# Splits of the fourth weight rows behind pair two's sums, pair three's tokens a step later, and two output scalings of the last pairs in another place

## The chip, the core and the metric

The kernel runs on one core of a Trainium2 chip. Five engines work side by side: TensorE multiplies matrices, VectorE (DVE in the profile) and ScalarE (ACT) work on tiles, GpSimd (POOL) does the small per-token numbers and some transfers, SyncE (SP) issues most transfers. Each engine runs its own instructions strictly in order and waits where an operand, a buffer or a transfer isn't ready. The metric is the device time of one execution in microseconds (us). The kernel before took 1026.99 us, the median of 3 runs (1026.68 to 1027.75).

## The reference, cut to what matters

One layer of a hybrid decoder: 2048 prompt tokens of width 1024 and 8 decode tokens. All is in fp32.

```python
def mixer_layer(x, pos, s_ret, s_hg, norm_g, w_in, ret_g, hg_g, lb, w_out):
    h = rmsnorm(x, norm_g)
    p = (h @ w_in).astype(jnp.float32)
    rq, rk, rv, rg, hq, hf, hi, hgate = jnp.split(p, 8, axis=-1)
    ...
    o_ret, s_ret_new = chunked_decay_recurrence(rq, rk, rv, log_gamma, s_ret)
    o_ret = head_rmsnorm(o_ret, ret_g) * jax.nn.silu(rg)
    ...
    o_hg, s_hg_new = chunked_decay_recurrence(hq_act, kin, hi, logf, s_hg)
    o_hg = head_rmsnorm(o_hg, hg_g) * jax.nn.silu(hgate)
    o_cat = jnp.concatenate([o_ret, o_hg], axis=-1).astype(x.dtype)
    y = x + o_cat @ w_out
    return y, s_ret_new, s_hg_new

y_prompt = rmsnorm(mixer_layer(x_prompt, ...), final_norm_g)
```

Two places matter here. The first is the value columns of `h @ w_in`, the first product that the kernel makes. The last is `x + o_cat @ w_out` with the final norm behind it, which ends the program.

## The kernel before, in words

**Number format.** Every fp32 operand of a product is split into a high and a low part. `hi_lo` (L116 to 118) does this: ScalarE copies the operand into a rounded tile (L117, names that end in `h`), and VectorE subtracts that from the operand (L118, names that end in `l`). `three` (L348 to 352) then issues three matmuls for every 128 rows of depth: high by high, high by the weight's low part, low by high.

**Pairs and seven products.** The prompt is worked in 8 pairs of two 128-token chunks. For a pair, tokens and weights form a 2 by 2 block product. It takes seven products in place of eight, in the order of `CHAIN` (L354): A11·B11 into bank a, A12·B21 into b, S2·T2 into a, S1·T1 into c, S3·T3 into a, S4·B22 into c, A22·T4 into a. A11 to A22 are blocks of the scaled tokens, S1 to S4 sums of them, B11 to B22 blocks of the weights, T1 to T4 sums of those. Each product is 12 matmuls of 512 columns. Banks a and c are used again within a pair: `keep` (L388 to 390) copies a bank's contents to SBUF with ScalarE after the first products (tiles `s`, `u`, `p`), and `emit` (L392) copies or adds out the finished results (L402, L403, L405).

**The first pairs.** Pairs 0 and 1 are done as eight plain products. Pair 2 is the first with seven, so the sums of the weights must stand ready by then. `wr[k]` are the rows of the weight as loaded, 8 blocks of 128; blocks `k` and `k + 4` meet in `wv_comb(k)` (L510), which makes T2, T3, T1, T4 by four VectorE subtractions in place (`w_sums`, L504 to 507) and splits each. `wv_comb(3)` (L688) makes the fourth such set. In pair 1's loop over its four banks, pair 2's tokens are prepared: `spread(2)` (L282) lays the norm factors of the tokens across the partitions (the copy at L290, tile `rb`); `tok_ops` (L295) scales eight token blocks with VectorE (L302), splits A (`ab_h`, `ab_l`; first A11 with 512 columns, then A12 and A22 together with 1024), and makes the sums S (L318 s1, L319 s2, L320 s3, L321 s4; s2 and s3 lie in one tile, s1 and s4 in another); `s_split` (L328) splits one of these tiles: `s20h`, `s20l` for S2 and S3, `s21h`, `s21l` for S1 and S4. SP stores the scaled tokens and the sums to DRAM for later passes (L312, L324).

**The loop over the further pairs.** From pair 2 on (L928 onward), work for other pairs is hung behind a pair's products: `after[n]` is called when the instructions of product n are written. In the program before, behind product 2 of pair `i` stand `tok_ops(i + 1)` and the split of its first sums, behind product 4 the split of the second; `tok_load(i + 2)` (L237) stands behind product 2 as well. For `i == 2` also `decode_values_out` (L609) stands behind product 3: four ScalarE copies of the decode tokens' values (L615) and two scalings (L616). `stats_sum` (L269) squares token rows `xn` on ScalarE for the norm factors.

**What sets the order.** TensorE's order is written out by hand. On the other engines a scheduler places each instruction. `behind(f)` (L126) holds what `f` issues behind the instructions last written on VectorE, ScalarE and SP, and `queued(f, engines)` (L1714) does so for the engines named.

**The output product.** At the end, `o_pair(i)` (L1799) makes the same seven products for `o_cat @ w_out`, in the order 0, 1, 2, 4, 5, 6, 3 (the last pair: 0, 1, 2, 4, 5, 3, 6). VectorE adds the results into the tiles `xro` of the pair's two chunks `ca` and `cb`, which hold `x` (loads at L1763, three buffers). `y_sq` squares them on ScalarE (L1767), `y_rs` makes the norm factor on GpSimd (L1770, L113, L114), and `y_out` (L1794) scales the finished 1024 columns on VectorE (L1796) and has GpSimd store them (L1797). A buffer of `xro` is free for the next load when that store is done. The last pair is put out in halves (`y_half`, L1789).

Of the kernel before, what the change touches and what calls it, by code (L numbers as in the profile page):

```python
# [14 lines left out]
ALU = mybir.AluOpType  # L15
# [26 lines left out]
def step_kernel(ctx, tc, a, out):  # L42
# [467 lines left out]
    def wv_comb(k):  # L510
        for op, r in w_sums(wr[k], wr[k + 4]):
            h, l = wv(op, k)
            hi_lo(h, l, r)

    def wg_load(n, k):
        for j, kk in enumerate((k, k + 4)):
            if n == 1 and (j or k % 2):
                tags = (f"zh{j}", f"zl{j}") if k % 2 else ("rk", "rg")
                wr[kk] = [vq.tile([P, GW], F32, tag=t, name=f"wgr{n}{kk}{t}") for t in tags]
                for g, r in enumerate(wr[kk]):  # L520
                    sp.dma_start(r, a[f"w_{n}"][kk, :, g * GW : (g + 1) * GW])
            else:
                wr[kk] = rawp.tile([P, 2, GW], F32, tag="raw", name=f"wgr{n}{kk}")
                sp.dma_start(wr[kk].rearrange("p g n -> p (g n)"), a[f"w_{n}"][kk])
# [160 lines left out]
    wv_comb(1)  # L685
    tok_load(2)
    wv_comb(2)
    wv_comb(3)  # L688
    for ty in (1, 0):
        for c in range(2):  # L690
            ps = bank([P, GW], f"pv1{c}{ty}")
            for k in range(KT):
                plain_k(1, ps, c, ty, k, k == 0, k == KT - 1)
            plain_out(1, c, ty, ps)
            if (c, ty) == (0, 0):
                spread(2)
                held = []
                stats_load(3, 0)
                stats_sum(3, 0)
                stats_load(3, 1)  # L700
                tok_ops(2, held, lambda: stats_sum(3, 1))
                stats_end(3)
                tok_load(3)
                for f in held:
                    f()
                s_split(2, 0)
    s_split(2, 1)
    stats_load(4, 0)
    dve.tensor_tensor(lbd, lbraw[:, :, 0], lbraw[:, :, 1], op=ALU.subtract)
    act.activation(lb, lbd, AF.Sigmoid)  # L710
# [208 lines left out]
    for i in range(2, n_tok):  # L919
# [16 lines left out]
        elif i + 1 < n_tok:  # L936
            if not spooled(i + 1):
                after[1] += [lambda i=i: spread(i + 1)]
            tied = behind if i >= N_V - 1 else lambda f: f()
            late = 2 if same(i) else 0  # L940
            after[2 + late] += [
                lambda i=i, t=tied: t(lambda: tok_ops(i + 1)), lambda i=i, t=tied: t(lambda: s_split(i + 1, 0))
            ]
            after[4 + late // 2] += [lambda i=i, t=tied: t(lambda: s_split(i + 1, 1))]
        if i + 2 < n_tok and not same(i + 2):
            at = 5 if i % N_V > 2 else 2
            if same(i + 1):
                at = 6
            after[at] += [lambda i=i: tok_load(i + 2)]
# [844 lines left out]
    def y_out(c, ms):  # L1794
        rows = slice(c * P, (c + 1) * P)
        dve.scalar_tensor_tensor(xro[c], xro[c], ms[:, 0:1], fg, op0=ALU.mult, op1=ALU.mult)  # L1796
        pool.dma_start(out["y_prompt"][0, rows, :], xro[c])  # L1797

    def o_pair(i, after):  # L1799
        ca, cb = 2 * i, 2 * i + 1  # L1800
        last = cb == T // P - 1
        box = {}
        lo, hi = slice(0, GW), slice(GW, D)
        ms = {c: sm.tile([P, 2], F32, tag="yms", name=f"yms{c}") for c in (ca, cb)}
# [5 lines left out]
        for step, n in enumerate((0, 1, 2, 4, 5, 3, 6) if last else (0, 1, 2, 4, 5, 6, 3)):  # L1810
# [11 lines left out]
                y_sq(ca, lo, ms[ca][:, 0:1])  # L1822
            elif n == 2:
                dve.tensor_tensor(keep("u2"), ps, box["s1"], op=ALU.add)  # L1824
            elif n == 4:
                dve.tensor_tensor(keep("u4"), ps, box["u2"], op=ALU.add)  # L1826
                dve.tensor_tensor(xa[:, hi], xa[:, hi], box["u4"], op=ALU.add)  # L1827
                dve.tensor_tensor(xb[:, hi], xb[:, hi], box["u4"], op=ALU.add)  # L1828
            elif n == 5:
                dve.tensor_tensor(xa[:, hi], ps, xa[:, hi], op=ALU.add)  # L1830
                y_sq(ca, hi, ms[ca][:, 1:2])
                y_rs(ms[ca])
                if not last:
                    y_out(ca, ms[ca])
                dve.tensor_tensor(xb[:, lo], xb[:, lo], box["u2"], op=ALU.add)  # L1835
            elif n == 3:
                dve.tensor_tensor(xb[:, hi], ps, xb[:, hi], op=ALU.add)
                dve.tensor_tensor(xb[:, lo], ps, xb[:, lo], op=ALU.add)
                if last:
                    y_sq(cb, hi, ms[cb][:, 0:1], D ** -0.5)  # L1840
                    pool.tensor_scalar(ms[cb][:, 0:1], ms[cb][:, 0:1], 1.0, EPS, op0=ALU.mult, op1=ALU.add)
                    queued(lambda: y_half(ca, ms[ca], hi), (dve,))
                else:
                    y_sq(cb, hi, ms[cb][:, 0:1])
                    y_sq(cb, lo, ms[cb][:, 1:2])
# [158 lines left out]
```

## Time and profile before

| | |
|---|---|
| median of 3 runs | 1026.99 us (1026.68 to 1027.75) |
| profiled execution's own time | 1027.67 us |
| its span, first to last instruction | 1025.8 us |
| TensorE granted clock, mean | 0.999 |
| busy: TensorE, VectorE, ScalarE, GpSimd | 1014.7, 734.3, 551.5, 126.3 us |
| DMA traffic | 255.63 MB, mean 249 GB/s |

The profiled execution has its own time, 1.9 us longer than its span: what lies before the first and behind the last instruction. A row of a timeline has start, length, engine, line, operation, output and inputs, sizes, the count of instructions in the row, and in brackets the engine's idle time just ahead with what ended it. A row with a count covers all its instructions from the first start to the last end. On TensorE and VectorE a listed length overlaps the start of the next instruction: in a run without waits, a 512-column matmul starts every 0.23 us though its row says 0.39. "PEclk" in a window is the share of TensorE's full clock that was granted.

### The profile page before, as it was taken

What the parts mean: (1) busy time and instruction counts of PE and PEld (TensorE: products, weight loads), DVE (VectorE), ACT (ScalarE), POOL (GpSimd) and SP (SyncE); (2) the same over time, 40 slices, a digit from 0 to 9 for tenths busy, and PEclk for the clock granted to TensorE, in tenths of its full rate; (3) what the DMA queues carried; (4) which work ended last, traced back from release to release, by engine and by line L of the source; (5) the groups of instructions that cost most, each with busy time, mean ns of one, the idle gap of its engine ahead of it and who ended that gap; (6) DMA issues with size and microseconds to landing.
All of it is one profiled execution on the core that took longest, in us unless ns stands there. A gap on an engine that the chain in (4) does not pass through costs nothing. (4 is left out here: it accounts for less than half of the span.)

```text
span 1025.8 us, 21565 instructions
## 1 busy us (share of the span) xinstructions
PE 1014.7 (99%) x8372; PEld 842.6 (82%) x8372; DVE 734.3 (72%) x1353; ACT 551.5 (54%) x1211; POOL 126.3 (12%) x231
## 2 busy tenths in 40 slices
PE   9999999999999999999999999999999999999996
PEld 8767778887778888888888899898888878887775
DVE  5897665988675885566666758768768576668886
ACT  6864335735434665555564655666556476433242
POOL 0210101000000101111111100111022112301122
PEclk9999999999999999999999999999999999999999
DMA  8688998768999975677776697655963497566652
GB/s 288 219 303 312 371 341 310 302 251 315 319 323 307 363 250 165 190 244 240 226 239 193 220 328 260 205 178 205 288 205 133 136 350 234 180 254 205 231 183 103
DMA packets 152135, 255.63 MB, mean 249 GB/s; under 512 B 11520, under 2 KB 79376, under 8 KB 151904
## 3 DMA queue, kind: packets, MB, share of 16 engines
q1 hardware_dynamic: 142232, 225.01, 64.7%
q0 software_dynamic: 7440, 24.76, 6.3%
q10 hardware_dynamic: 2360, 4.47, 1.2%
q8 instruction: 66, 1.08, 0.4%
q14 instruction: 37, 0.30, 0.1%
HBM read 166.51 MB, written 87.69 MB: 248 GB/s over the span
## 5 line engine op out<-in xcount | busy, mean ns | idle before, releaser
L1054 PE MATMUL pjfh<-xh,w_h 128*128 128x512 f32 (+2 forms) x160 | 59.4, 371 | 0.0
L1054 PE MATMUL pjqh<-xh,w_h 128*128 128x512 f32 (+2 forms) x160 | 58.7, 367 | 0.0
L1248 ACT ACTIVATE kepth<-kh 128x1024 f32<-128x1024 f32 x24 | 25.4, 1060 | 60.4 <-DVE kh L1238 60.4
L1054 PE MATMUL pjfh<-xl,w_h 128*128 128x512 f32 (+2 forms) x160 | 55.7, 348 | 0.0
L1054 PE MATMUL pjqh<-xh,w_l 128*128 128x512 f32 (+2 forms) x160 | 55.7, 348 | 0.0
L1054 PE MATMUL pjfh<-xh,w_l 128*128 128x512 f32 (+2 forms) x160 | 55.6, 348 | 0.0
L1054 PE MATMUL pjqh<-xl,w_h 128*128 128x512 f32 (+2 forms) x160 | 55.6, 347 | 0.0
L1238 DVE TENSOR_TENSOR kh<-kh,fph 128x512 f32<-128x512 f32 x48 | 33.4, 696 | 22.7 <-PE plh L1268 19.7
L118 DVE TENSOR_TENSOR ab_l<-xr,ab_h 128x512 fp32r<-128x512 f32 (+1 forms) x40 | 37.4, 954 | 14.1 <-ACT ab_h L117 14.1
L783 DVE SCALAR_TENSOR_TENSOR obr<-por,omr,rg 128x128 f32<-128x128 f32 x64 | 18.0, 344 | 31.9 <-POOL omr L775 24.9
L773 ACT ACTIVATE obr<-por 128x128 f32<-128x128 f32 x64 | 16.9, 278 | 44.1 <-PE por L760 40.3
L117 ACT ACTIVATE ab_h<-xr 128x512 fp32r<-128x512 f32 (+1 forms) x40 | 32.3, 839 | 8.4 <-DVE xr L302 8.4
L1054 PEld LDWEIGHTS pjqh<-xh,w_h 128*128 128x128 f32 x160 | 30.4, 190 | 4.8 <-issue 1.2
L1054 PEld LDWEIGHTS pjfh<-xh,w_h 128*128 128x128 f32 x160 | 30.2, 189 | 4.1 <-issue 0.4
L1054 PEld LDWEIGHTS pjqh<-xh,w_l 128*128 128x128 f32 x160 | 30.1, 188 | 4.0
L1054 PEld LDWEIGHTS pjfh<-xh,w_l 128*128 128x128 f32 x160 | 30.1, 188 | 4.0
L409 ACT ACTIVATE vo<-vo 128x512 f32<-128x512 f32 x32 | 20.1, 629 | 23.7 <-DVE vo L403 10.5
L1241 DVE TENSOR_TENSOR qqh<-qqh,fph 128x512 f32<-128x512 f32 x48 | 32.8, 683 | 0.0
L1054 PEld LDWEIGHTS pjqh<-xl,w_h 128*128 128x128 f32 x160 | 30.2, 189 | 3.0
L1054 PEld LDWEIGHTS pjfh<-xl,w_h 128*128 128x128 f32 x160 | 30.2, 189 | 2.7
L302 DVE SCALAR_TENSOR_TENSOR xr<-xr,g_in,rb 128x256 f32<-128x256 f32 x64 | 26.9, 479 | 2.6 <-DMA xr<-in_x_t 2.4
L1681 PE MATMUL py<-woh,oc_h 128*128 128x512 f32 x64 | 26.7, 417 | 0.0
(1877 smaller groups left out, 3347.0 us busy)
## 6 DMA issues: line engine op xcount, KB each, us to landing
xr<-a_dram SPq DMA_DIRECT2D x24, 512.0 KB
S<-s_dram SPq DMA_DIRECT2D x24, 512.0 KB
xn<-in_x_prompt SPq DMA_DIRECT2D x32, 256.0 KB
xr<-in_x_t SPq DMA_DIRECT2D x16, 512.0 KB
a_dram<-xr SPq DMA_DIRECT2D x16, 512.0 KB
s_dram<-S SPq DMA_DIRECT2D x16, 512.0 KB
xr<-a_dram SPq DMA_DIRECT2D x32, 256.0 KB
or<-o_dram SPq DMA_DIRECT2D x16, 512.0 KB
```

What stands on the lines that cost most here:

```text
L117: act.activation(h, src, AF.Copy)
L118: dve.tensor_tensor(l, src, h.bitcast(F32), op=ALU.subtract)
L302: dve.scalar_tensor_tensor(r[:, k], r[:, k], g_in[:, kk : kk + 1], spread_to[i], op0=ALU.mult, op1=ALU.mult)
L409: act.activation(o, src, AF.Silu)
L773: act.activation(o[:, cc], po[:, h], AF.Square, scale=P ** -0.5, accum_out=ms[:, h : h + 1])
L783: dve.scalar_tensor_tensor(o[:, cc], po[:, h], ms[:, h : h + 1], rb_of[c, "g"][:, cc], op0=ALU.mult, op1=ALU.mult)
L1054: pe.matmul(ps, ww[:, kk], x[:, k, b0 : b0 + n], start=(k == 0 and i == 0), stop=(k == KT - 1 and i == 2),)
L1238: dve.tensor_tensor(kv[:, :, 0, :], kv[:, :, 0, :], two[:, :, 1:2].to_broadcast([P, nb, b]), op=ALU.mult)
L1241: dve.tensor_tensor(qv[:, :, 1, :], qv[:, :, 1, :], two[:, :, 0:1].to_broadcast([P, nb, b]), op=ALU.mult)
L1248: act.activation(ss[:, 512:], k[:, :HALF], AF.Copy)
L1681: pe.matmul(ps, o[:, kk], w[:, k % 4, i * 512 : (i + 1) * 512], start=(k == 0 and n == 0), stop=(k == KT - 1 and n == 2),)
```

## The change

It has three parts.

First, the fourth set of weight sums. `wv_comb_two(3)` makes three of the four subtractions and splits T2 where `wv_comb(3)` stood. T1's split is given to `behind` after the split of pair 2's first sums, and T3's split, the fourth subtraction and T4's split to `behind` after the split of the second.

Second, for `i == 2` the token work of pair 3 and its first split stand behind product 3 in place of 2, and `tok_load(4)` likewise. The second split stays behind product 4.

Third, in pair 6 the scaling and the store of chunk 12 are queued on VectorE behind the additions of product 3, and those of chunk 13 are kept for the last pair, queued behind its `u2` addition (L1824).

```diff
+    def wv_comb_two(k):
+        b11, b12, b21, b22 = (r[:, g] for r in (wr[k], wr[k + 4]) for g in range(2))
+        dve.tensor_tensor(b11, b12, b11, op=ALU.subtract)
+        dve.tensor_tensor(b12, b22, b12, op=ALU.subtract)
+        dve.tensor_tensor(b22, b22, b11, op=ALU.subtract)
+        hi_lo(*wv("T2", k), b22)
+        def one():
+            hi_lo(*wv("T1", k), b11)
+        def two():
+            hi_lo(*wv("T3", k), b12)
+            dve.tensor_tensor(b21, b21, b22, op=ALU.subtract)
+            hi_lo(*wv("T4", k), b21)
+        return one, two
...
-    wv_comb(3)
+    comb_t1, comb_t34 = wv_comb_two(3)
...
                 s_split(2, 0)
+                behind(comb_t1)
     s_split(2, 1)
+    behind(comb_t34)
...
-            late = 2 if same(i) else 0
+            late = 2 if same(i) else 1 if i == 2 else 0
...
-            at = 5 if i % N_V > 2 else 2
+            at = 5 if i % N_V > 2 else 3 if i == 2 else 2
...
+    y_late = []
...
             elif n == 2:
                 dve.tensor_tensor(keep("u2"), ps, box["s1"], op=ALU.add)
+                if last:
+                    queued(y_late.pop(), (dve,))
...
-                if not last:
+                if not last and not before_last:
                     y_out(ca, ms[ca])
...
+                elif before_last:
+                    queued(lambda: y_out(ca, ms[ca]), (dve,))
+                    y_sq(cb, hi, ms[cb][:, 0:1])
+                    y_sq(cb, lo, ms[cb][:, 1:2])
+                    y_rs(ms[cb])
+                    y_late.append(lambda: y_out(cb, ms[cb]))
```

The orders of TensorE and SP are the same in both kernels. The rows below are pieces of the programs' order on one engine; a row has line, operation, output, inputs and size. Lines of the changed kernel stand 17 to 30 further down in the later parts of the program (L402 to L405 keep theirs, L615 becomes L632, L1796 becomes L1815).

**Around pair 2's sums.** ScalarE before, from the split of S2 and S3 to the copy `u` behind product 4:

```order
L117 ACTIVATE s20h<-S_2_710 128x1024
L117 ACTIVATE s21h<-S_2_711 128x1024
L390 ACTIVATE s_2_792<-pv2a 128x512
L269 ACTIVATE xn_763,ms_821<-xn_763 128x512
L117 ACTIVATE ab_h<-xr_719 128x512
L390 ACTIVATE u_2_840<-pv2a 128x512
```

The same piece in the changed kernel:

```order
L117 ACTIVATE s20h<-S_2_703 128x1024
L117 ACTIVATE T1h<-wvr_292 128x512
L117 ACTIVATE s21h<-S_2_704 128x1024
L117 ACTIVATE T3h<-wvr_292 128x512
L390 ACTIVATE s_2_792<-pv2a 128x512
L269 ACTIVATE xn_763,ms_821<-xn_763 128x512
L117 ACTIVATE T4h<-wvr_294 128x512
L390 ACTIVATE u_2_840<-pv2a 128x512
```

T1h and T3h now stand ahead of the copy `s` of bank a, and T4h ahead of `u`; all three stood far ahead of pair 2's tokens before. The first split of pair 3's tokens (`ab_h<-xr_719`) has left this piece. VectorE before, ahead of pair 2's tokens:

```order
L506 TENSOR_TENSOR wvr_294<-wvr_294,wvr_292 128x512
L118 TENSOR_TENSOR T1l<-wvr_292,T1h 128x512
L507 TENSOR_TENSOR wvr_294<-wvr_294 128x512
L118 TENSOR_TENSOR T3l<-wvr_292,T3h 128x512
L118 TENSOR_TENSOR T2l<-wvr_294,T2h 128x512
L118 TENSOR_TENSOR T4l<-wvr_294,T4h 128x512
L290 COPY rb_683<-prs_680 128x256
```

VectorE after, first the same place and then the place to which the four went:

```order
L519 TENSOR_TENSOR wvr_294<-wvr_294,wvr_292 128x512
L118 TENSOR_TENSOR T2l<-wvr_294,T2h 128x512
L290 COPY rb_676<-prs_673 128x256
L302 SCALAR_TENSOR_TENSOR xr_568<-xr_568,g_in,rb_676 128x256 x4
L302 SCALAR_TENSOR_TENSOR xr_569<-xr_569,g_in,rb_676 128x256 x2
```

```order
L118 TENSOR_TENSOR s20l<-S_2_703,s20h 128x1024
L118 TENSOR_TENSOR T1l<-wvr_292,T1h 128x512
L118 TENSOR_TENSOR s21l<-S_2_704,s21h 128x1024
L118 TENSOR_TENSOR T3l<-wvr_292,T3h 128x512
L527 TENSOR_TENSOR wvr_294<-wvr_294 128x512
L405 TENSOR_TENSOR vo_807<-pv2b,s_2_792 128x512
L290 COPY rb_819<-prs_816 128x256
L118 TENSOR_TENSOR T4l<-wvr_294,T4h 128x512
```

Four VectorE instructions left the place ahead of `rb` and stand among the low parts of pair 2's sums and pair 3's `rb`.

**Around pair 3's tokens.** ScalarE before, from the last square before the tokens to the copy of bank a at L402, which the seventh product of pair 2 waits for:

```order
L269 ACTIVATE xn_764,ms_821<-xn_764 128x512
L117 ACTIVATE ab_h<-xr_720 128x1024
L390 ACTIVATE p_2_890<-pv2c 128x512
L117 ACTIVATE s30h<-S_3_856 128x1024
L615 ACTIVATE vd_892<-pvd 8x256 x2
L615 ACTIVATE vd_897<-pvd 8x256 x2
L402 ACTIVATE vo_914<-pv2a 128x512
```

And in the changed kernel:

```order
L269 ACTIVATE xn_764,ms_821<-xn_764 128x512
L117 ACTIVATE ab_h<-xr_712 128x512
L390 ACTIVATE p_2_860<-pv2c 128x512
L117 ACTIVATE ab_h<-xr_713 128x1024
L117 ACTIVATE s30h<-S_3_876 128x1024
L632 ACTIVATE vd_892<-pvd 8x256 x2
L632 ACTIVATE vd_897<-pvd 8x256 x2
L402 ACTIVATE vo_914<-pv2a 128x512
```

The 512-column split came between `xn_764` and `p`, and the 1024-column split moved from ahead of `p` to behind it. VectorE before, where the sums of pair 3 are made:

```order
L318 TENSOR_TENSOR S_3_857<-xr_719,xr_720 128x512
L320 TENSOR_TENSOR S_3_856<-xr_719 128x512
L319 TENSOR_TENSOR S_3_856<-S_3_857,xr_719 128x512
L118 TENSOR_TENSOR ab_l<-xr_720,ab_h 128x1024
L321 TENSOR_TENSOR S_3_857<-xr_720,S_3_856 128x512
L118 TENSOR_TENSOR s30l<-S_3_856,s30h 128x1024
```

And in the changed kernel:

```order
L118 TENSOR_TENSOR ab_l<-xr_712,ab_h 128x512
L318 TENSOR_TENSOR S_3_877<-xr_712,xr_713 128x512
L118 TENSOR_TENSOR ab_l<-xr_713,ab_h 128x1024
L319 TENSOR_TENSOR S_3_876<-S_3_877,xr_712 128x512
L320 TENSOR_TENSOR S_3_876<-xr_712 128x512
L321 TENSOR_TENSOR S_3_877<-xr_713,S_3_876 128x512
L118 TENSOR_TENSOR s30l<-S_3_876,s30h 128x1024
```

The two subtractions that fill the tile of `s30h` (L319 and L320) stood ahead of the long `ab_l` and stand behind it now.

**In the last pairs.** VectorE before, from the last subtraction of chunk 13 to the addition of `u2` into chunk 15 (`xro_10935` is chunk 12, `xro_10937` chunk 13, `xro_11115` chunk 14, `xro_11117` chunk 15):

```order
L1849 TENSOR_TENSOR xro_10937<-xro_10937,po_11097 128x512
L1796 SCALAR_TENSOR_TENSOR xro_10935<-xro_10935,yms_10967,fg 128x1024
L118 TENSOR_TENSOR op7S1l<-oS_7_11033,op7S1h 128x1024
L1837 TENSOR_TENSOR xro_10937<-po_11119,xro_10937 128x512
L1838 TENSOR_TENSOR xro_10937<-po_11119,xro_10937 128x512
L1796 SCALAR_TENSOR_TENSOR xro_10937<-xro_10937,yms_10968,fg 128x1024
L118 TENSOR_TENSOR op7A22ob<-or_10986,op7A22ks 128x512
L1819 TENSOR_TENSOR xro_11115<-xro_11115,os_7_11162 128x512
L1821 TENSOR_TENSOR xro_11115<-po_11165,xro_11115 128x512
L1824 TENSOR_TENSOR ou_7_11194<-po_11181,os_7_11162 128x512
L1835 TENSOR_TENSOR xro_11117<-xro_11117,ou_7_11194 128x512
```

And in the changed kernel (chunk 14 is `xro_11113`, chunk 15 `xro_11115` there):

```order
L1879 TENSOR_TENSOR xro_10937<-xro_10937,po_11095 128x512
L118 TENSOR_TENSOR op7S1l<-oS_7_11033,op7S1h 128x1024
L1861 TENSOR_TENSOR xro_10937<-po_11117,xro_10937 128x512
L1862 TENSOR_TENSOR xro_10937<-po_11117,xro_10937 128x512
L1815 SCALAR_TENSOR_TENSOR xro_10935<-xro_10935,yms_10967,fg 128x1024
L118 TENSOR_TENSOR op7A22ob<-or_10986,op7A22ks 128x512
L1841 TENSOR_TENSOR xro_11113<-xro_11113,os_7_11160 128x512
L1843 TENSOR_TENSOR xro_11113<-po_11163,xro_11113 128x512
L1846 TENSOR_TENSOR ou_7_11192<-po_11179,os_7_11160 128x512
L1815 SCALAR_TENSOR_TENSOR xro_10937<-xro_10937,yms_10968,fg 128x1024
L1859 TENSOR_TENSOR xro_11115<-xro_11115,ou_7_11192 128x512
```

The scaling of chunk 12 moved behind two additions, that of chunk 13 behind four more instructions. GpSimd before, from the norm factor of chunk 12 to the store of chunk 13:

```order
L114 TENSOR_TENSOR yms_10967<-yms_10967,mhalf 128x1
L1797 DMA out_y_prompt<-xro_10935 128x1024
L1770 TENSOR_TENSOR yms_10968<-yms_10968 128x1
L113 TENSOR_SCALAR yms_10968<-yms_10968 128x1
L114 TENSOR_TENSOR yms_10968<-yms_10968,mhalf 128x1
L1797 DMA out_y_prompt<-xro_10937 128x1024
```

And in the changed kernel:

```order
L114 TENSOR_TENSOR yms_10967<-yms_10967,mhalf 128x1
L1789 TENSOR_TENSOR yms_10968<-yms_10968 128x1
L113 TENSOR_SCALAR yms_10968<-yms_10968 128x1
L114 TENSOR_TENSOR yms_10968<-yms_10968,mhalf 128x1
L1816 DMA out_y_prompt<-xro_10935 128x1024
L1816 DMA out_y_prompt<-xro_10937 128x1024
```

The store of chunk 12 now stands behind the three instructions of chunk 13's norm factor.

1 line of the change is left out of this document (added).

## The prediction

> **What bounds the kernel now.** I read the busy times, then what TensorE waited for, then the timelines of the engines that it waited for, then the last 25 us.
>
> ```profile
> PE 1014.7 (99%) x8372; PEld 842.6 (82%) x8372; DVE 734.3 (72%) x1353; ACT 551.5 (54%) x1211; POOL 126.3 (12%) x231
> ...
> PE pv2a L350 <- ACT ab_h L117: 0.9, 1, 0.9
> PE pv2c L350 <- ACT p L390: 0.6, 1, 0.6
> PE pv2a L350 <- ACT s L390: 0.3, 1, 0.3
> ```
>
> TensorE is busy 99% of the span. Beside one wait at the start, these three and the 0.24 us at 60.66 below are all the waits that the view lists for it, 2.1 us together, and all lie in pair 2. Where TensorE never waits, a later start passes through to its end undiminished, so the sum has two places only: pair 2, and the tail behind the last matmul.
>
> ```profile
> 60.66 0.50 PE L350 MATMUL pv2b<-wv_h,ab_l 128*128 128x512 f32 x1 [0.24 <-DVE ab_l L118]
> ...
> 63.79 0.50 PE L350 MATMUL pv2a<-T2h,s20h 128*128 128x512 f32 x1 [0.33 <-ACT s L390]
> ...
> 73.25 0.50 PE L350 MATMUL pv2c<-B22h,s21h 128*128 128x512 f32 x1 [0.64 <-ACT p L390]
> ...
> 76.27 0.50 PE L350 MATMUL pv2a<-T4h,ab_h 128*128 128x512 f32 x1
> ```
>
> The last row starts pair 2's seventh product. It shows no wait now, and it is the one by which I measure pair 2: from there TensorE runs without a wait, and whatever moves 76.27 moves the end.
>
> **The change part by part. First: the splits that left the place ahead of pair 2's tokens.**
>
> ```profile
> 53.23 0.68 DVE L118 TENSOR_TENSOR T4l<-wvr,T4h 128x512 fp32r<-128x512 f32 x1
> 53.84 0.41 DVE L290 COPY rb<-prs 128x256 f32<-128x256 f32 x1
> ...
> 59.39 1.22 DVE L118 TENSOR_TENSOR ab_l<-xr,ab_h 128x1024 fp32r<-128x1024 f32 x1
> 60.53 0.68 DVE L319 TENSOR_TENSOR S<-S,xr 128x512 f32<-128x512 f32 x1
> ```
>
> From start to start a 512-column VectorE instruction costs 0.60 us (53.23 to 53.84) and a 1024-column one 1.14 (59.39 to 60.53). Four of 0.60 go: 2.4 us. But T2l still waits for T2h:
>
> ```profile
> 51.28 0.62 ACT L117 ACTIVATE T2h<-wvr 128x512 fp32r<-128x512 f32 x1
> ...
> 55.99 0.63 ACT L117 ACTIVATE ab_h<-xr 128x512 fp32r<-128x512 f32 x1 [1.57 <-DVE xr L302]
> 56.53 0.61 ACT L269 ACTIVATE xn<-xn 128x512 f32<-128x512 f32 x1
> ...
> 57.14 0.61 ACT L269 ACTIVATE xn<-xn 128x512 f32<-128x512 f32 x1
> ...
> 58.18 1.06 ACT L117 ACTIVATE ab_h<-xr 128x1024 fp32r<-128x1024 f32 x1 [0.33 <-DVE xr L302]
> ...
> 61.24 1.06 ACT L117 ACTIVATE s20h<-S 128x1024 fp32r<-128x1024 f32 x1 [1.43 <-DVE S L319]
> 62.21 1.04 ACT L117 ACTIVATE s21h<-S 128x1024 fp32r<-128x1024 f32 x1
> 63.16 0.58 ACT L390 ACTIVATE s<-pv2a 128x512 f32<-128x512 f32 x1
> ```
>
> T2h can come only some 0.3 us sooner (its sum is made first, the square ahead of it stays), so it ends at 51.65, T2l starts there, and `rb` at 52.3: 1.55 us earlier than 53.84. The first `ab_h` then comes at 54.4, and TensorE's first stall (0.9 us, about 1.2 with the slower first matmuls behind it) is gone. The long `ab_h` gains less: it stands behind the square at 57.14, whose tile SP asks for here:
>
> ```profile
> 53.88 0.33 SPq L263 DMA_DIRECT2D xn<-in_x_prompt  x1
> ```
>
> That load follows the release of its buffer, which the change leaves where it is, so I keep the square at about 56.9 and the long `ab_h` at 57.55: 0.63 earlier. The long `ab_l` follows at 58.65, and the matmul of 60.66 comes at 59.9, 0.7 earlier. The sum L319 starts at 59.85 and `s20h` at 60.5. Now ScalarE has T1h and T3h ahead of `s`: 0.54 each by the 512-column row (55.99 to 56.53), with 0.97 for each 1024-column split (61.24 to 62.21). `s` starts at 60.5 + 2 x 0.97 + 2 x 0.52 = 63.45 in place of 63.16. So the product at 63.79 comes at 64.1: **0.3 later, and all that the front gained is given back.** `p` now comes in time, so product six starts behind its predecessor at 73.25 - 0.8 + 0.3 = 72.75, 0.5 earlier.
>
> **Second: pair 3's tokens.** What the seventh product waits for is the copy of bank a at L402, on ScalarE:
>
> ```profile
> 71.04 0.63 ACT L269 ACTIVATE xn<-xn 128x512 f32<-128x512 f32 x1 [2.48 <-DMA xn<-in_x_prompt]
> ...
> 71.67 1.04 ACT L117 ACTIVATE ab_h<-xr 128x1024 fp32r<-128x1024 f32 x1
> 72.62 0.58 ACT L390 ACTIVATE p<-pv2c 128x512 f32<-128x512 f32 x1
> 73.10 1.05 ACT L117 ACTIVATE s30h<-S 128x1024 fp32r<-128x1024 f32 x1
> 74.05 1.54 ACT L615 ACTIVATE vd<-pvd 8x256 f32<-8x256 f32 x4
> 75.61 0.60 ACT L402 ACTIVATE vo<-pv2a 128x512 f32<-128x512 f32 x1
> ```
>
> Call the start of the square X. Before, X = 71.04 and the seventh product starts X + 0.63 (square) + 0.95 (`ab_h`) + 0.48 (`p`) + 0.95 (`s30h`) + 1.56 (`vd`) + 0.60 (copy) + 0.06 = X + 5.23. That chain is ScalarE's alone, and fits tightly: bank a is read 0.6 us before the product.
>
> In the changed order the 512-column split comes in (0.54), and `s30h` waits for VectorE: the long `ab_h` ends 1.06 after its start, then the long `ab_l` (1.14), L319 (0.60) and L320 (0.68) follow on VectorE with 0.05 for each of two handovers. X + 0.63 + 0.54 + 0.48 + 1.06 + 0.05 + 1.14 + 0.60 + 0.68 + 0.05 + 0.95 + 1.56 + 0.60 + 0.06 = X + 8.40. At the same X the seventh product is 3.2 us later. What is hidden nowhere is the 2.4 us that ScalarE stands still for VectorE, with `vd` and the copy queued behind `s30h`, and TensorE waiting for the copy.
>
> X itself is a transfer:
>
> ```profile
> 62.34 1.03 SPq L263 DMA_DIRECT2D xn<-in_x_prompt  x1
> ...
> 55.00:62.00 7.00, 5.86 (x24) 3.91 (x23) 6.87 (x13) 4.25 (x8) 1.95 (x3) 1.00 0.86 317
> 62.00:76.00 14.00, 13.03 (x57) 9.86 (x55) 12.44 (x21) 8.41 (x18) 0.00 (x0) 1.00 0.99 342
> ```
>
> It is asked for at 62.34, behind the stores of pair 2's sums, which come 0.7 earlier; the DMA engines are full here (share 0.99 from 62 to 76), so it takes its 8.7 us. I take X = 70.3. The seventh product then starts at 78.7, **2.4 us late**. The later bound is an unchanged X, 3.2 late. The earlier one is VectorE, whether or not the load is early:
>
> ```profile
> 68.83 0.88 DVE L302 SCALAR_TENSOR_TENSOR xr<-xr,g_in,rb 128x256 f32<-128x256 f32 x2
> ```
>
> The scalings end at 69.70 now. Four instructions of 0.60 come ahead of them, one `ab_l` (0.60) leaves, and the chain starts 0.7 earlier: 70.8. The long `ab_h`, X + 1.65, can't be sooner, which makes X worth 69.2 and the product 77.6: 1.3 late. T4l and T4h are ready some 8 us before they are read, and cost nothing beside these terms. The few other places where rows trade places in pairs 3 to 6 have TensorE ahead of no wait in the trace; I cost them at nothing, at most 0.3 late.
>
> **Third: the last pairs.**
>
> ```profile
> 1003.10 1.28 DVE L1796 SCALAR_TENSOR_TENSOR xro<-xro,yms,fg 128x1024 f32<-128x1024 f32 x1 [0.94 <-POOL yms L114]
> ...
> 1006.03 0.68 DVE L1838 TENSOR_TENSOR xro<-po,xro 128x512 f32<-128x512 f32 x1
> 1008.86 1.28 DVE L1796 SCALAR_TENSOR_TENSOR xro<-xro,yms,fg 128x1024 f32<-128x1024 f32 x1 [2.14 <-POOL yms L114]
> ...
> 1012.78 0.69 DVE L1835 TENSOR_TENSOR xro<-xro,ou 128x512 f32<-128x512 f32 x1
> ...
> 1018.72 0.68 DVE L1849 TENSOR_TENSOR xro<-xro,po 128x512 f32<-128x512 f32 x1
> ...
> 1017.71 0.39 PE L350 MATMUL po<-woh,op7A22ob 128*128 128x512 f32 x1
> ```
>
> Here VectorE, not TensorE, is late: it waits 0.94 and 2.14 us for GpSimd's norm factors. Both waits go, since the two additions at 1005.43 and 1006.03 come 2.2 us sooner and four instructions stand ahead of chunk 13's scaling. But chunk 15's buffer is that of chunk 12, and hangs on its store:
>
> ```profile
> 1004.79 0.66 POOL L1797 DMA_DIRECT2D out_y_prompt<-xro  x1 [1.73 <-DVE xro L1796]
> ...
> 1007.82 0.33 SPq L1763 DMA_DIRECT2D xro<-in_x_prompt  x1
> ...
> 1010.75:1011.50 0.75, 0.75 (x5) 0.63 (x4) 0.65 (x2) 0.00 (x0) 0.42 (x1) 1.00 0.00 0
> ```
>
> The store is issued at 1004.79, the load 3.03 later, and its last bytes come near 1011.07 (the window behind shows no traffic), 3.25 after issue. Now the store waits on GpSimd behind chunk 13's norm factor, to about 1006.65; load 1009.7, landing 1012.93, and the addition of 1012.78 at 1012.96: **0.2 later.** VectorE loses its waits and finds this one. Were the load in time, the tail would gain until the last matmul binds: it ends at 1018.10, so the row of 1018.72 can't start before 1018.15, a gain of 0.57. A slower load costs up to 0.8, by the same sum with the store 0.6 later. The sum: 2.4 + 0.2 = **2.6 us later**. The profiled execution's own 1027.67 becomes 1030.3. That execution was 0.68 above the median, so I forecast 1026.99 + 2.6 = **1029.6 us**.
>
> **A rule against the row.** TensorE stands idle about 3.1 us ahead of the seventh product. In both windows of pair 2 above the granted clock is 1.00, but the longest gap in them is 0.9 us. The Trainium skill, "TensorE: Matmul & The Clock Gate", Part 1, says that an idle window of about 3.4 us halves the clock, and that it takes as long a busy one to restore it. No row here shows such a gap, so the rule enters as a rival only. With its price the sum is that rival's, without it the forecast's.
>
> **The rivals.** *The transfer is early (other side).* Everything that VectorE does for pair 2 comes earlier, so SP may get its loads out earlier too. If the tile of the square at 57.14 came 1 us sooner than I have it, the long `ab_h`, the sums and with them VectorE's scalings of pair 3 would all come 1 us sooner; with X early as well, the bound of 1.3 late would fall to 0.3, and with chunk 15's load in time the tail gains 0.57: 1026.99 + 0.3 - 0.57 = 1026.7. It is on the faster side from 0.73 us of earlier tile on. For it speaks that the first `ab_h` stores its tokens sooner, against it the full DMA engines, and that nothing in SP's order ahead of that load changes. 17%. *All four stalls go.* If the copy at L402 is not held by `s30h`, the 2.1 us of stalls with their slow first matmuls, 3.3 in all, and the tail's 0.6 are gained: 1023.1. The order of ScalarE speaks against it, since the copy stands behind `s30h` and `vd`. 5%. *The gap slows the clock.* If a 3 us gap halves the granted clock for 3.4 us, 15 matmuls of 0.23 us become 7.5: 1.7 us more, 1031.3. 10%. *The change doesn't do what it says:* the rows of its order show that it does, so no chance is kept for that.
>
> **How the numbers follow.** A measurement of this kernel tells about 0.2% from no change, 2.05 us; so slower begins at 1029.04 and faster at 1024.94. The forecast has 68%. Its own range runs from 1.3 - 0.6 = 0.7 to 3.2 + 0.8 = 4.0 late, 1027.7 to 1031.0; about seven tenths of it lie over 2.05. Slower: 0.48 + 0.10 = 0.58. Within: 0.17 + 0.19 = 0.36. Faster: 0.06, the early case's best end added to the 5%. The range goes down to 1026.4, which takes in the early transfer with 0.3 to spare, and up to 1031.0; left out are the vanished stalls, part of the slow clock.
>
> **What would show it.** Right: TensorE's waits name `s` (about 1.6 us: bank b's product, begun at 58.35 without the first stall and held to 59.9 by the long `ab_l`, ends near 62.5, ahead of 64.1), `ab_l` (1.1) and, at the seventh product, the copy L402 with some 3 us, with `s30h` starting right behind L320; the row of `ab_h` at 55.99 without a stall behind it. In the tail, no scaling waits for GpSimd, and the addition of chunk 15 waits about 3 us for a DMA. Wrong: a seventh product within 1 us of 76.27, a wait of TensorE behind pair 3, or a square (X) before 69. If X stays at 71.04 the time is nearer to 1030.4.

## The result, and the profile after

The changed kernel took 1035.46 us, the median of 7 runs (1030.80 to 1036.76), against 1026.99 us before (7 runs, 1026.42 to 1030.48): a ratio of 1.007, with a 95% interval of 1.0055 to 1.0085. That is 7.2 us slower by the means of the runs (1034.81 against 1027.56) and 8.5 by the medians. The direction is that of the forecast, the size is not: 1029.6 was forecast and 1031.0 was the upper end.

The first execution profiled is the fastest of the seven, 1030.80. TensorE's waits in it are few (columns: us in total, times, longest):

```profile
PE pv2a L350 <- ACT vo L402: 3.4, 1, 3.4
PE pv2a L350 <- ACT s L390: 1.4, 1, 1.4
PE wu L84 <- POOL ones L78: 1.1, 1, 1.1
PE pv L350 <- DVE wv_l L118: 0.2, 1, 0.2
```

Three of the four waits in pair 2 are gone, `s` waits longer, and there is a new one of 3.4 us for the copy at L402. ScalarE's timeline of the same execution shows what holds that copy:

```profile
69.29 0.63 ACT L269 ACTIVATE xn<-xn 128x512 f32<-128x512 f32 x1 [2.86 <-DMA xn<-in_x_prompt]
...
69.92 0.62 ACT L117 ACTIVATE ab_h<-xr 128x512 fp32r<-128x512 f32 x1
70.44 0.58 ACT L390 ACTIVATE p<-pv2c 128x512 f32<-128x512 f32 x1
70.92 1.05 ACT L117 ACTIVATE ab_h<-xr 128x1024 fp32r<-128x1024 f32 x1
74.46 1.06 ACT L117 ACTIVATE s30h<-S 128x1024 fp32r<-128x1024 f32 x1 [2.50 <-DVE S L320]
75.43 1.53 ACT L632 ACTIVATE vd<-pvd 8x256 f32<-8x256 f32 x4
76.98 0.60 ACT L402 ACTIVATE vo<-pv2a 128x512 f32<-128x512 f32 x1
```

ScalarE stands for 2.50 us at `s30h`, and `vd` and the copy stand behind it. TensorE in the same execution, on both sides of the gap:

```profile
73.87 0.39 PE L350 MATMUL pv2c<-B22h,s21l 128*128 128x512 f32 x1
77.64 0.79 PE L350 MATMUL pv2a<-T4h,ab_h 128*128 128x512 f32 x1 [3.38 <-ACT vo L402]
78.23 0.63 PE L350 MATMUL pv2a<-T4l,ab_h 128*128 128x512 f32 x1
78.65 0.63 PE L350 MATMUL pv2a<-T4h,ab_l 128*128 128x512 f32 x1
...
82.49 0.63 PE L350 MATMUL pv2a<-T4h,ab_l 128*128 128x512 f32 x1
...
84.18 0.50 PE L350 MATMUL pv3a<-wv_h,ab_h 128*128 128x512 f32 x1
```

And its windows, whose columns from the right are GB/s, DMA share and granted clock:

```profile
74.00:76.00 2.00, 0.26 (x2) 0.00 (x0) 1.48 (x3) 1.52 (x3) 0.00 (x0) 1.00 0.84 344
76.00:78.00 2.00, 0.36 (x1) 0.37 (x2) 1.94 (x4) 1.94 (x5) 0.00 (x0) 0.65 1.04 383
78.00:80.00 2.00, 2.00 (x6) 1.52 (x6) 1.53 (x2) 1.75 (x5) 0.17 (x1) 0.50 1.02 178
80.00:82.00 2.00, 2.00 (x6) 1.58 (x5) 0.00 (x0) 0.00 (x0) 0.91 (x3) 0.50 0.88 333
82.00:84.00 2.00, 2.00 (x19) 0.65 (x17) 0.14 (x1) 0.00 (x0) 0.00 (x0) 0.65 1.00 386
```

The matmuls of the seventh product start every 0.42 to 0.43 us (78.23 to 78.65) where 0.23 is usual, and the granted clock is 0.50: the clock was halved in the gap, and stayed so for the whole product. A mean of 0.65 over 2 us means 1.4 us at half clock, so the slow stretch lasted about 6.8 us, from 76.6 to 83.4. Before, pair 3 starts 3.93 us after the seventh product (76.27 to 80.20); here it takes 6.54.

This execution is not typical. A later one of the same kernel, 1034.76 us, is near the median, and its ratio to the profiled execution of before (1034.76 / 1027.67 = 1.0069) is that of the runs above. It ran on another chip, whose medians are 1033.61 us against 1027.82.

| us | before | changed, 1030.80 | changed, 1034.76 |
|---|---|---|---|
| X, square behind the awaited load | 71.04 | 69.29 | 70.90 |
| seventh product of pair 2 starts | 76.27 | 77.64 | 79.25 |
| pair 3 starts | 80.20 | 84.18 | 85.65 |
| last matmul ends | 1018.10 | 1021.90 | 1023.66 |
| last matmul to the end of the span | 7.71 | 7.12 | 9.32 |
| span | 1025.81 | 1029.02 | 1032.98 |

The 7.2 us between the first column and the last are 3.0 for the later seventh product (79.25 - 76.27), 2.5 for the halved clock behind it (6.40 - 3.93), 0.1 from there to the last matmul, and 1.6 behind the last matmul. In the faster execution they are 1.4, 2.6, -0.2 and -0.6. The experiments test the first, the second and the last of these terms.

### The profile page after: what moved, and what is told of

Read it like the earlier page. It is cut to its first block, busy times and chain, and to the rows that moved or that the text cites. A ratio compares the mean times of both kernels' runs of the same rounds, so it can differ in the third digit from the quotient of the medians.

```text
span 1029.0 us, 21571 instructions
## 1 busy us (share of the span) xinstructions
PE 1015.7 (99%) x8372; PEld 844.1 (82%) x8372; DVE 734.7 (71%) x1353; ACT 552.4 (54%) x1211; POOL 128.2 (12%) x231
## 4 chain that ended last, share of the span: by engine, by line
PE 91%; DMA 5%; ACT 2%; DVE 1%; issue 1%; SPq 0%; POOLq 0%; POOL 0%; ACTq 0%
PE po L350 11%; PE pjqh L1073 9%; PE pjfh L1073 8%; PE py L1700 4%; DMA xn<-in_x_prompt 4%; PE plh L1287 2%; PE puh L1156 1%; PE pur L771 1%; PE par L764 1%; PE por L777 1%; PE poh L1172 1%; PE por L779 1%; PE poh L1174 1%; PE pv20a L350 1%; PE pv22a L350 1%; PE pv21a L350 1%
## 5 line engine op out<-in xcount | busy, mean ns | idle before, releaser
L792 ACT ACTIVATE obr<-por 128x128 f32<-128x128 f32 x64 | 16.9, 278 | 44.4 <-PE por L779 40.6
```

## The experiments

Ratios are to the kernel before on the same chip. A difference from 1 counts as shown where the interval behind the ratio leaves out 1. "Tail" is the time from the last matmul's end to the end of the span.

**Each part alone.** Of the changed kernel's three parts, two at a time were taken out.

```diff
-            late = 2 if same(i) else 1 if i == 2 else 0
+            late = 2 if same(i) else 0
-            at = 5 if i % N_V > 2 else 3 if i == 2 else 2
+            at = 5 if i % N_V > 2 else 2
```

This takes out the second part; the first is undone by `wv_comb(3)` in its old place, the third by `y_out` in its old places.

> First part alone (the fourth weight set split late; tokens and tail as before). Theory (the loss is one gap: ScalarE's copy of bank a at L402 stands behind pair 3's split s30h, TensorE idles 3.4 us ahead of pair 2's seventh product and its clock is then halved): here s30h stands behind the copy, so the seventh product starts within 0.5 us of its predecessor's end, near 74.2 in place of 76.27, clock 1.00 throughout; about 2 us faster than before, near 1025. Rival (the late T1, T3 and T4 splits themselves are the loss): a gap of over 2 us in pair 2 and a time over 1029.

> Second part alone (pair 3's tokens and the load a step later). Theory: without the weight splits between, ScalarE's and VectorE's order in pair 2 stays that of before but for one small instruction, so the seventh product stays within 0.3 us of 76.27 and the time within 1 us of before, near 1027. Rival (the later token step is by itself the loss, whatever the splits do): s30h waits behind the long ab_l, the seventh product comes near 79 with a halved clock behind it, 1031 or more.

> Third part alone (chunks 12 and 13 scaled later in the last pairs). By the trace of the changed kernel the stretch from the last pairs' matmuls to the end is 0.8 us shorter than before: 0.5 to 0.9 us faster, near 1026.3, with pair 2 as before. Rival (chunk 12's store behind chunk 13's norm factor makes the last load late): 0.2 or more slower, the addition of chunk 15 waiting for its load longer than VectorE had to spare.

The first part alone: 0.9979 (0.9969 to 0.9990), 1026.21 us against 1027.97. The second alone: 0.9995 (0.9983 to 1.0007). The third alone: 1.0001 (0.9988 to 1.0014), where 0.5 to 0.9 us of gain were expected: a miss, taken up below. **No part is slow by itself.** ScalarE with the first part alone:

```profile
69.76 0.63 ACT L269 ACTIVATE xn<-xn 128x512 f32<-128x512 f32 x1 [1.33 <-DMA xn<-in_x_prompt]
...
73.39 0.60 ACT L402 ACTIVATE vo<-pv2a 128x512 f32<-128x512 f32 x1
73.89 1.05 ACT L117 ACTIVATE s30h<-S 128x1024 fp32r<-128x1024 f32 x1
```

Here the copy stands ahead of `s30h`, and the seventh product starts at 74.34 without a wait. With the second part alone `s30h` stands ahead of the copy, as before the change, but the sums that it splits are ready in time (`s30h` at 72.27, copy at 74.78). Only the two together put it ahead of the copy and make its input late.

**The one place in ScalarE's order.** In the changed kernel, pair 3's first split was written behind product 5.

```diff
-                lambda i=i, t=tied: t(lambda: tok_ops(i + 1)), lambda i=i, t=tied: t(lambda: s_split(i + 1, 0))
+                lambda i=i, t=tied: t(lambda: tok_ops(i + 1))
             ]
+            after[4 if i == 2 else 2 + late] += [lambda i=i, t=tied: t(lambda: s_split(i + 1, 0))]
```

> The changed kernel with one thing moved: pair 3's first split (s30h) stands behind product 5 of pair 2 in place of product 3, which puts it behind the copy L402 on ScalarE. Theory: the copy then starts at X + 4.2 (X the start of the awaited square, 69.3 to 70.3), the seventh product comes at 74 to 75.2, the gap falls from 3.4 to under 1 us and the clock stays at 1.00: 1024 to 1025.5, faster than before. Rival (the loss is from the DMA or the late splits, not from this one place in ScalarE's order): the gap stays above 2 us or the halved clock stays, 1030 or more.

0.9994 (0.9982 to 1.0005), 1026.79 us: this one move takes back the whole loss, but no gain on before is shown, where 1024 to 1025.5 was expected: a miss. X was 70.59 in its profile and the seventh product came at 75.38, X + 4.79, where the expected copy at X + 4.2 makes X + 4.86; so the load still sets it. Its slowest two runs had a mean clock of 0.996.

A mean clock doesn't say where the clock was slow, since it also counts the idle time behind the last matmul. In the profile of 1035.74 us below, the clock is 0.50 from about 1025 to the end of the span, 8.9 us, and that alone takes 0.004 off the mean. A long tail and a slow stretch behind the gap therefore look alike in it, and only a profile tells them apart.

**What the gap costs, and what the clock.** The changed kernel once more, and beside it one with TensorE busy in the gap; then the kernel before with a gap put into it, by copies that are made two times (as below) or four times (`* 4`).

```diff
+            if i == 2 and n == 5:
+                again = ps_tr.tile([P, GW], F32, tag="tr", name="again")
+                for k in range(4):
+                    three(again, av(i, x, k), wv(w, k), k == 0, k == 3)
```

```diff
-            for n in range(2):
+            for n in list(range(2)) * 2:
                 j = 2 * ty + n
                 act.activation(t[:, n * 256 : n * 256 + 256], pvd[0][32 * j : 32 * j + NB], AF.Copy)
```

> The changed kernel as it is, again, beside the three below. Theory (the seventh product starts at X + 8.4, X being the landing of the awaited tile, and every landing later than in the first profile passes through; the gap ahead of it halves the clock for some 6 us): median 1033 to 1036, mean clock 0.995 or less in nearly all runs, and if the profiled one is slower than 1031, the gap is longer by the same amount and X later by it. Rival (the slower runs lose their time elsewhere): the gap is 3.4 us as in the first profile whatever the time.

> The changed kernel with pair 2's sixth product issued a second time into a bank that nobody reads: 12 matmuls, 2.7 us of TensorE work in the gap, all else alike. Theory (the halved clock behind the gap costs 2.6 us or more): the seventh product starts where it did (77.6 if X is the same), the clock is 1.00 behind it, its 12 matmuls run at 0.23 us: 2.5 to 4 us faster than the changed kernel of the same call, mean clock 0.998. Rival (the gap is only a wait and the clock nothing): the same time as the changed kernel, or longer.

> The kernel before with each of the four copies of the decode tokens' values on ScalarE made twice, ahead of the copy L402: 1.56 us more there, nothing else. It opens a gap of 1.6 us ahead of pair 2's seventh product. Theory (a gap costs its length, and the clock falls only behind a gap of about 3 us): clock 1.00 behind the gap, the seventh product at X + 6.8, 1.6 us slower than before. Rival (any gap there slows the clock): matmuls at 0.43 us behind it, 4 us slower.

> The same with each copy made four times: 4.7 us more, a gap of about 4.7 us. Theory: the seventh product at X + 9.9, matmuls at 0.43 us for some 5 to 6 us behind it, so 4.7 plus about 2.5 from the clock: 7 us slower than before, mean clock 0.995. Rival (the halved clock of the changed kernel has another cause, such as its late weight splits): clock 1.00, 4.7 us slower.

The changed kernel again: 1.0049 (1.0033 to 1.0065), mean clock 0.994 to 0.996 in its six runs. Its profile is the last column of the table. The gap is 3.5 us, hardly longer than the first one; X is 1.6 later and the seventh product 1.6 later, since TensorE's product ahead of it was nearly as late (72.68 against 71.38). So what parts these two executions is not the gap's length, as the expectation had it, but the front of the program and the tail.

The window behind the seventh product's start (78.49, 76.80, 79.52) in three profiles, the granted clock third from the right: first the filled gap, where TensorE still waits 0.72 us for the copy.

```profile
80.00:84.00 4.00, 4.00 (x30) 2.58 (x29) 2.35 (x4) 0.60 (x2) 1.08 (x3) 1.00 0.94 324
```

Then the kernel before with the gap of 1.6 us (a wait of 1.62).

```profile
80.00:84.00 4.00, 4.00 (x30) 2.89 (x23) 2.77 (x4) 0.16 (x1) 0.25 (x1) 1.00 0.93 340
```

Then with that of 4.8 us (a wait of 4.82).

```profile
80.00:84.00 4.00, 4.00 (x11) 3.03 (x11) 1.42 (x2) 1.63 (x5) 1.08 (x3) 0.50 0.76 269
```

With the gap filled, the seventh product starts as late (X + 8.35, as in the changed kernel), yet the clock is 1.00 and pair 3 starts 3.93 us after it, as before the change: in the profiles 2.5 us are the clock's. The times of the runs don't confirm the size. In the median the filled version gained only 1.0 us on the changed kernel (1032.63 against 1033.61) where 2.5 to 4 were expected, and its ratio (1.0046, 1.0034 to 1.0058) is not told apart from 1.0049. Its tail was 9.64 us in the profile, and three of its five runs had a mean clock of 0.996; whether they lost it in the tail or elsewhere is not shown, since only the first of the five was profiled. The gap of 1.6 us left the clock at 1.00 and gave a ratio of 1.0012 (1.0001 to 1.0023); that of 4.8 us halved it in the kernel before too, pair 3 starting 6.18 us after the seventh product: 1.006 (1.0043 to 1.0077). One of its four runs took 2043.51 us, which nothing here explains and the ratio leaves out; the other three lie from 1032.03 to 1034.39. So the halved clock needs nothing of the change but its gap.

**The load that X hangs on.** Its issue on SP was put ahead of pair 3's token loads and of the stores of pair 2's sums, in the changed kernel and in one without the second part.

```diff
                 stats_end(3)
-                tok_load(3)
+                stats_load(4, 0)
+                behind(lambda: tok_load(3))
...
-    stats_load(4, 0)
```

> The changed kernel with the load of the awaited tile (and its first half) issued ahead of pair 3's token loads and of the stores of pair 2's sums. Theory: X leaves the chain; what is left is VectorE's scalings, which end near 69.5, then 6.75 us of split, sums and copies: the seventh product near 76.3, a gap of 2 to 2.5 us without a halved clock, 1026 to 1027.5, and runs closer together. Rival (the load is not what the copy at L402 hangs on): no change against the changed kernel, 1033 or more.

> First and third part of the change without the later tokens, and with the earlier load. Theory: s30h stands behind the copy L402 and X is out of the chain, so the seventh product follows its predecessor at 74.1 in every run: 1.6 to 3 us faster than before in the median, 1024 to 1025.5 where before has 1027 to 1028, and less scatter. Rival (before's scatter has another source than this load): the median is that of the first part alone, and the scatter as wide as before's.

The first: 1.002 (1.0005 to 1.0035), seventh product at 77.04 behind a wait of 2.1 us, at a clock of 1.00, with `s30h` waiting for VectorE. That is the kind of bound that was expected, 0.7 us later than the 76.3 worked out. The median, 1029.31, is about 2 us over the 1027.5 at which the expected range ends. In five of the twelve runs the mean clock was still 0.996 or less; where they lost it is not shown. The second: 0.9988 (0.9978 to 0.9999), seventh product at 73.64, no gap at all; but its scatter (1025.68 to 1029.76) is nearly that of before on that chip (1025.94 to 1030.60), which the expectation had blamed on this load. That half of the expectation falls.

**The tail.** The changed kernel with its third part taken out (twice), as it is, and with chunk 12's store put first on GpSimd.

```diff
-                    y_rs(ms[cb])
+                    queued(lambda: y_rs(ms[cb]), (pool,))
                     y_late.append(lambda: y_out(cb, ms[cb]))
```

> First and second part of the change without the third (the last pairs as before). Theory (in the executions in which VectorE is late in the last pairs, chunk 12's store behind chunk 13's norm factor makes the last load late and costs 1.6 us; in the others the last matmul binds and nothing differs): half a us to 1.6 faster than the changed kernel, 5 to 6 us slower than before, and from the last matmul to the end no more than 7.8 us. Rival (the third part costs nothing): the changed kernel's ratio, 1.005 to 1.007.

> The changed kernel beside the two below, to be compared with them on one chip. Both theories: a seventh product at X + 8.4, a halved clock behind it, ratio to before 1.005 to 1.007.

> First and second part without the third, beside the changed kernel. Theory (the third part costs, when VectorE is late): median 1 to 2.5 us under the changed kernel of this call, and 7.1 to 7.8 us from the last matmul to the end. Rival (the third part costs nothing, and the earlier difference of the two was that of chips): within 0.7 us of it.

> The changed kernel with GpSimd's norm factor of chunk 13 tied behind the store of chunk 12, nothing else. Theory (what the third part costs is the late store of chunk 12, and with it the last load): the median falls to that of the version without the third part or below it, and chunk 15's addition waits less for its load. Rival (the cost of the third part is something else in the last pairs, or none): within 0.7 us of the changed kernel.

Without the third part: 1.0029 (1.0020 to 1.0038), on another chip than the changed kernel's 1.0049, so it was repeated on one: the changed kernel 1.0064 (1.0049 to 1.0079), without the third part 1.0033 (1.0018 to 1.0047), with the store first 1.0032 (1.0021 to 1.0043). **The third part costs about 3 us in the changed kernel** (1034.77 us in the median against 1031.61 without it), more than the 1 to 2.5 expected, **and within these intervals all of that is chunk 12's late store** (1031.65 with the store first). The addition of chunk 15 in the changed kernel (the profile of 1035.74 us), with the store and the load ahead of it:

```profile
1012.14 0.66 POOL L1816 DMA_DIRECT2D out_y_prompt<-xro  x1
1014.77 0.53 POOL L1816 DMA_DIRECT2D out_y_prompt<-xro  x1 [1.97 <-DVE xro L1815]
...
1015.17 0.33 SPq L1782 DMA_DIRECT2D xro<-in_x_prompt  x1
...
1020.95 0.69 DVE L1859 TENSOR_TENSOR xro<-xro,ou 128x512 f32<-128x512 f32 x1 [6.58 <-DMA xro<-in_x_prompt]
```

And with the store first on GpSimd:

```profile
1008.64 0.66 POOL L1816 DMA_DIRECT2D out_y_prompt<-xro  x1 [2.11 <-DVE xro L1815]
...
1011.68 0.33 SPq L1782 DMA_DIRECT2D xro<-in_x_prompt  x1
...
1015.04 0.69 DVE L1859 TENSOR_TENSOR xro<-xro,ou 128x512 f32<-128x512 f32 x1 [1.04 <-DMA xro<-in_x_prompt]
```

From store to load 3.0 us in both; from the load to the addition 5.8 against 3.4. In the first, chunk 13's store (1014.77) goes out just ahead of the load. All ten profiles with the third part in agree with that order as the cause: where chunk 13's store was issued behind the load, the addition starts 3.3 to 3.8 us after the load's issue (seven profiles), and where it was issued ahead of it, 4.0, 4.5 and 5.8 us (three). No run changed this order alone, so it is not shown that the store slows the load. With the store first, the wait falls from 6.58 to 1.04 us and the tail from 10.94 to 7.13. Whether a late store shows depends on where VectorE stands. The start of chunk 13's last subtraction ahead of the last matmul's end tells it:

| profile | ahead, us | tail, us |
|---|---|---|
| third part in: 1030.80, third part alone | 18.7, 18.5 | 7.12, 7.12 |
| third part in: 1034.76, 1035.74, filled gap | 17.0, 16.7, 16.9 | 9.32, 10.94, 9.64 |
| third part out: before, without it (two) | 16.6, 18.3, 16.1 | 7.71, 7.12, 8.17 |
| store first | 18.9 | 7.13 |

Where VectorE is 18.3 us or more ahead, the last matmul binds in every order (7.12); at 18.1 and 18.2 (the earlier load, the later split) the changed order has 7.49 and 7.36. Where it is 16 to 17 ahead, the old order costs 0.6 to 1.1 and the changed one 2.2 to 3.8. The profile of the third part alone caught the first kind, and its runs show no loss. Of the seven profiles with a halved clock three are of the late kind and four are not, and two at full clock, before and the filled gap, are late ones too; what sets this distance, no run here tells.

**A version that is faster.** The first part with the earlier load, without the third part, and with the third part and the store first.

> First part of the change alone with the earlier load of the awaited tile, the last pairs as before. Theory: the seventh product at 73.7 as with the third part in, and the tail at 7.1 to 7.8 us in every run: faster than before by 0.2 to 0.35%, so at least as good as the first part alone (ratio 0.998). Rival (the third part is worth something beside an early pair 2): no better than the version with it, ratio 0.9988.

> First and third part with the earlier load, and with chunk 12's store first on GpSimd. Theory: the seventh product at 73.7, 7.1 us from the last matmul to the end; faster than before by 0.2 to 0.35%, at least as good as without the third part (ratio 0.9983 on another chip). Rival: no better than 0.9988, the same version with the late store.

0.9983 (0.9975 to 0.9992), 1026.17 us against 1028.09, and 0.9989 (0.9979 to 0.9999). The first is faster than both kernels, by 0.17% against before, a little less than the 0.2 to 0.35% expected. It isn't told apart from the first part alone (0.9979), so neither the earlier load nor the third part is shown to be worth anything beside it.

## Why the prediction was right or wrong, point by point

**The place and the mechanism: right.** The seventh product was said to start at X + 8.40, behind the copy at L402, which waits for `s30h`, which waits for L320. It started at X + 8.33 to 8.35 in the three profiles of the changed kernel, and `s30h` waited 2.50 us for L320 (the prediction's text says 2.4, its own terms add up to 2.5). X was taken as 70.3 and was 69.29, 70.90 and 70.37. The one move of the split that answers to this step takes back the loss.

**The front: right in kind, mis-sized.** The first stall is gone, that for `p` is gone or 0.2 us, and `s` waits 1.3 to 1.4 us, 1.6 forecast. The stall of 1.1 us for `ab_l` was 0.4 or less, because that square's load came earlier than assumed (56.19 for the long split in the first profile, 57.55 forecast). So the product that waits for `s` came at 62.70, 63.83 and 63.08, where before has 63.79 and 64.1 was forecast. That alone gains nothing at the end: the seventh product waits for the copy at L402, and where TensorE arrives there earlier, the gap is longer.

**The clock: the step that failed.** "TensorE stands idle about 3.1 us ahead of the seventh product" was right (3.4 and 3.5 us in the two profiles), but the sum was made at full clock, and the gap's effect entered only as a rival with a chance of 10%, priced at 1.7 us. Measured, it is there in every profile of the changed kernel, and costs 2.6, 2.5 and 1.6 us. In its place: a wait of 3.4 us already halves the clock, for about 6.8 us in the first two of these profiles (part of it within the gap) and about 3.4 us in the third. The price of 1.7 us was right for the short stretch and too low for the long one. The row that was weighed against it, a clock of 1.00 around a gap of 0.9 us, said nothing about one more than three times as long. The Trainium skill, "TensorE: Matmul & The Clock Gate", Part 1, has the idle window at about 3.4 us and the busy one as long. The traces agree: 3.4 us of waiting sufficed in all seven profiles that have such a wait, 1.6 and 2.1 did not, and the slow stretch lasted about 3.4 us in three of the seven and about 6.8 in four.

**The tail: mis-sized.** The term was +0.2 with an upper end of +0.8. The chain was the right one (chunk 12's store behind chunk 13's norm factor, load, landing, addition of chunk 15), and both scalings' waits went, as said. But it measured 1.6 and 3.2 us in two of three profiles, -0.6 in the third, and about 3 us between the runs with and without it on one chip. The store was put at 1.86 us later by taking GpSimd's three small instructions at the lengths they have before; they grew (next section but one). The load, taken to land 3.25 us after issue, took up to 5.8 us from its issue to the addition. The 3.25 itself was misread: the row given for it shows no traffic from 1010.75 on, 2.9 us after issue. That it lies close to the 3.3 to 3.8 us of the undisturbed loads is luck. In the first profile VectorE was 2 us further ahead, which the prediction had no term for: it took VectorE's distance from TensorE as fixed, from one execution.

**The rivals.** The vanished stalls did not come. The early transfer came in part: the tile of the square was 1.3, 0.2 and 1.0 us sooner than forecast (squares at 55.56, 56.68 and 55.93 against 56.9), and VectorE's scalings ended sooner too (69.45, 70.57 and 69.83 against 70.8). But X, for which the long `ab_h` waited in all three profiles, was 1.0 us sooner than taken in the first and no sooner in the others, so the seventh product was 1.4 us late at best and not 0.3. The chance of slower, 0.58, was too low for the same reason as the range was: a mechanism known and priced was left out of the sum and its bounds. That the fastest execution, 1030.80 us, lies near the forecast is luck: its seventh product was 1.4 us late where 2.4 was forecast and its tail 0.6 shorter, and these made up for the clock's 2.6.

## What to carry to other kernels

Where a change opens a gap on TensorE, work out its length and compare it with the longest wait that profiles show at full clock (2.1 us here) and the shortest that halved it (3.4 us here). From there on the cost is the gap and, on top of it, the slow clock behind it, 1.3 to 2.7 us in these profiles; in between nothing is measured, so the slow stretch belongs at least into the range. An instruction on an in-order engine that frees a bank must not stand behind one whose input another engine makes late; here two harmless moves made that together. And where an engine's lead over another is not fixed by a wait, take it from several executions, since what a later store costs hangs on it.

## What the runs showed of the hardware

A small GpSimd instruction can take as long as VectorE's work beside it. Before, L113 on one column runs while VectorE stands idle; in the changed kernel it falls beside a 1024-column subtraction with two SBUF inputs. Before:

```profile
1002.23 0.19 POOL L113 TENSOR_SCALAR yms<-yms 128x1 f32<-128x1 f32 x1
```

Changed, with VectorE's row:

```profile
1003.78 1.22 DVE L118 TENSOR_TENSOR op7S1l<-oS,op7S1h 128x1024 fp32r<-128x1024 f32 x1
...
1003.93 1.11 POOL L113 TENSOR_SCALAR yms<-yms 128x1 f32<-128x1 f32 x1
```

It takes 1.11 us in place of 0.19, and ends near the end of VectorE's instruction. The Trainium skill, "SBUF — State Buffer", section "SBUF: two separate sides", says that the two engines share one pair of ports, held by one of them for a whole instruction; these rows agree.

The clock also does not always fall in the gap: in the profile of 1035.74 us the first four matmuls of the seventh product ran at full pace, and those behind them started 0.43 us apart. The same windows as above show it there:

```profile
78.00:80.00 2.00, 1.29 (x5) 1.07 (x6) 1.69 (x4) 1.98 (x4) 0.00 (x0) 0.89 1.08 289
80.00:82.00 2.00, 2.00 (x6) 1.54 (x5) 0.86 (x1) 0.82 (x4) 0.93 (x3) 0.50 0.72 233
82.00:84.00 2.00, 2.00 (x20) 1.00 (x18) 0.10 (x1) 0.00 (x0) 0.14 (x1) 0.76 1.01 394
```

The half clock adds up to about 3.4 us here (0.4, 2.0 and 1.0), against 6.8 in the first profile. So behind gaps of nearly the same length, 3.38 and 3.53 us of waiting, the slow stretch differed by a factor of two, and with it the cost (1.6 against 2.6 us).
